# Projecting attention's q and k together in seven half-size products

## The chip, the cores and the metric

The program runs on one core of a Trainium2 chip. The metric is the time of one execution on the device in microseconds. The engines are called by the profile's names: PE (TensorE, the matmuls), DVE (VectorE), ACT (ScalarE), POOL (GpSimd) and SP (SyncE, which issues most of the transfers).

## The reference

One decoder block on 512 tokens of width 1024, all in float32:

```python
h = rmsnorm(x, g_mix)
z = h @ w_in   # q_r,k_r (256 each), v_r,g_r (512 each), q_f,k_f,v_f (512 each), f_f (8), a_r,a_f (1024 each)
o_r = groupnorm(retention(rot(q_r), rot(k_r), v_r)) * g_ret_norm       # chunks of 128 tokens, 4 heads
y_r = (silu(g_r) * o_r) @ w_ret_o
q_f, k_f = rmsnorm(q_f per head, g_q), rmsnorm(k_f per head, g_k)      # 8 heads of 64
y_f = forgetting_attention(q_f, k_f, v_f, logsigmoid(f_f + b)) @ w_fox_o   # causal softmax, bias from cumulative sums of f
x = x + (sigmoid(a_r) * y_r + sigmoid(a_f) * y_f) @ w_out
x = x + (silu(h2 @ w_gate) * (h2 @ w_up)) @ w_down,   h2 = rmsnorm(x, g_ffn)
```

## The kernel before

Each float32 factor is split into a high part (a cast to a shorter format, on ACT) and a low part (the factor less its high part, on DVE); a product of two factors is three matmuls: high by high, high by low, low by high. A *split* of a weight tile of 128 x 1024 is thus one ACT cast (`wh`, line 162) and one DVE subtraction (`wl`, line 163).

The projections of h are done with x scaled by g_mix in `xh`, `xl`; the norm's factor `rstd1` of each token is multiplied in when a result leaves its bank. They come in this order on PE:

1. q_r and k_r together, 512 columns, while x is being loaded.
2. v_r and g_r as a pair, in seven products of half size instead of eight, by a scheme like Strassen's (Winograd's form). The left factor x is cut in four blocks A11, A12, A21, A22 (token halves by alternate row tiles of the width), the weights of the two outputs make the blocks B11, B12, B21, B22 (`blk0` to `blk3`, four buffers of the pool `bp`). Sums of x's blocks (`s1` to `s4`) and sums of weight blocks (line 385, 422) are split and multiplied, and results are added up in the banks `x_`, `y_`, `z_` and in copies `u`. Each product is 24 matmuls of 512 columns (4 row tiles, 2 token tiles, 3 parts).
3. q_f with the 8 forget columns (two column halves of 256 and 264, 96 matmuls each), k_f and v_f (96 matmuls of 512 columns each), by `tok_group`; then the sigmoid gates a_r, a_f (`gates`), then `y_ret`, the projection of retention's output.

The third part does not run by itself. It is a generator `fill`, and a hand-written order takes matmuls worth so many microseconds from it between the steps of retention (rotations on POOL in `ret_rotate`, transposes, scores, values, group norm) and later of the forgetting attention (`fox_...`). The numbers `RF`, `CF`, `PF`, `SF`, `VF`, `TAIL` say how much goes between which steps. While `pinned` is set, PE's instructions keep the order in which they are written; DVE, ACT and POOL are ordered by the framework's scheduler, except where `after` or `queue` chains two instructions. SP issues transfers in the written order while `moves` is set.

Retention runs chunk by chunk (t = 0 to 3): `ret_turn` transposes the rotated q, k (`rot` to `rT`), `ret_scores` makes scores (`sT`) and the state's update (`kv`, `sn`), `ret_values` the outputs in two banks, `ret_norm` statistics and the scaled output `og`, `ret_out` multiplies by the gate `gs` and transposes. q_f and k_f are normalised per head on POOL, turned on DVE (`turn_heads`), written to DRAM and read back head by head (`put_heads`, `get_heads`). In the attention stage the softmax weights are turned on DVE and through DRAM into `pT` (`fox_turn`, `fox_put`, `fox_get`) before `fox_values` multiplies them with v_f.

Of the kernel before, what the change touches and what calls it, by code (L numbers as in the profile page):

```python
# [17 lines left out]
P = 128  # L18
# [34 lines left out]
def block_kernel(ctx: ExitStack, tc, x, xT, c_early, c_tab, c_late, w_qf, w_tok, w_vg, w_a, w_y, w_o, w_gu, w_gl, w_dn, w_dh, out):  # L53
# [88 lines left out]
    RF, CF, PF, SF, LAG = (5.72, 4.64, 5.6, 4.6, 11.2), (3.0, 2.0, 2.26, 4.0), 5.9, (0.63, 0.83, 1.57, 1.4), 2  # L142
# [57 lines left out]
    for k in range(NK):  # L200
# [6 lines left out]
        loads = (load, nc.sync.dma_start(out=raw, in_=w_tok[2, u, :, cs]))  # L207
# [26 lines left out]
    def load_block(b):  # L234
        for v in range(2):
            nc.sync.dma_start(out=blocks[b][:, v, :], in_=w_vg[b, v])
# [33 lines left out]
    def tok_group(src, evac, cuts=(512,), done=(), behind=None):  # L270

        u = 0
        for c, w in enumerate(cuts):
            accs = [bank("acc") for _ in range(NT)]
            kpu = 1024 // (w // 256 * 256)
            for k in range(NK):
                if k % kpu == 0:
                    h, l = done[u] if u < len(done) else split_w(src(u, w * kpu), w * kpu)
                    if behind is not None and u == len(done):
                        after(split_raw.last[0], behind)  # L280
                    u += 1
# [45 lines left out]
    def unit(group):  # L327
        return lambda u, width: w_tok[group, u]

# [7 lines left out]
    def x_sum(n, p, q, op, behind=None):  # L337
# [7 lines left out]
        h = bp.tile([P, 4, HS], F32R, name="sh", tag="sh", bufs=2)  # L345
        l = bp.tile([P, 4, HS], F32R, name="sl", tag="sl", bufs=2)
# [83 lines left out]
    def x_low(n):  # L430
        h = bp.tile([P, 4, HS], F32R, name="sh", tag="sh", bufs=2)
        l = bp.tile([P, 4, HS], F32R, name="sl", tag="sl", bufs=2)
# [26 lines left out]
    t3.append(half(B12, 1))  # L459
    products(x_, t3, s3, False)  # L460
# [4 lines left out]
    b6.append(half(B22, 1))  # L465
    products(z_, b6, s4, False)
# [3 lines left out]
    for v in range(2):  # L470
        sum_half(B11, v, B21)
    b7 = [half(B11, v) for v in range(2)]
    last_low = turn_of[0]
    for tp in range(2):
        queue(tt(out=vr[:, tp, :], in0=y_[tp], in1=us[tp][:, 0, :], op=ALU.add))
    queue_q = split_raw(load_w(w_qf[0, :, :1024]))
    queue(split_raw.last[1])
# [26 lines left out]
    bp.release()  # L504
    orp = tc.alloc_tile_pool(name="orp", bufs=1, side="right")
    sgp = tc.alloc_tile_pool(name="sgp", bufs=1, side="right")


    orh = orp.tile([P, RH, S], F32R, name="orh")
    orl = orp.tile([P, RH, S], F32R, name="orl")  # L510
# [80 lines left out]
    def ret_norm(t):  # L591
# [10 lines left out]
        rsqrt(r4, mv[:, :, 1], 1.0, [P, RH], "n4")  # L602
        og = rwk.tile([P, 512], F32, name="og", tag="og")
        for h in range(RH):
            hs = slice(h * P, (h + 1) * P)
            ts(out=og[:, hs], in0=o[h], scalar1=mv[:, h, 0:1], scalar2=r4[:, h:h + 1], op0=ALU.subtract, op1=ALU.mult)
        ret[t].update(og=og)

    def ret_out(t):
        og = ret[t]["og"]  # L610
        after(gp.tensor_tensor(out=gs[:, t, :], in0=gs[:, t, :], in1=gret, op=ALU.mult), ret[1]["rotated"])
        tt(out=og, in0=og, in1=gs[:, t, :], op=ALU.mult)
# [16 lines left out]
    def head_norm(z, g=None):  # L629
# [3 lines left out]
        def one(t):  # L633
# [3 lines left out]
            if t == NT - 1:  # L637
                r8 = sm.tile([P, NT, FH], F32, name="r8", tag="r8")
                rsqrt(r8.rearrange("p t h -> p (t h)"), s8.rearrange("p t h -> p (t h)"), 1.0 / FD, [P, NT * FH], "n8")
                for u in range(NT):  # L640
                    z3 = z[:, u, :].rearrange("p (h d) -> p h d", h=FH)
                    gp.tensor_tensor(out=z3, in0=z3, in1=r8[:, u, :].rearrange("p (h o) -> p h o", o=1).broadcast_to([P, FH, FD]), op=ALU.mult)
                    if g is not None:
# [916 lines left out]
```

## Time and profile before

| | |
|---|---|
| median of 3 runs | 682.74 us (682.62 to 683.54) |
| profiled execution | 682.73 us, span 680.9 us |
| granted PE clock | 0.999 |
| PE matmul busy | 673.2 us, 3399 records |
| DVE / ACT / POOL busy | 535.5 / 351.0 / 76.2 us |

A row of the timeline gives the start, the duration, the engine, the line of the kernel, the operation, `out<-in` tiles, and in brackets the idle time before it with what ended it. Rows of one engine can overlap by their pipeline, so the distance between two starts is the better price. In the stretches the columns are the length, then busy time and instructions of PE, PEld, DVE, ACT and POOL, the granted clock, the DMA share and GB/s. A wait's row gives the total, the times and the longest.

### The profile page before, as it was taken

Reading aid. Unit: us, or ns where it says so; the run is one execution under the profiler, and the core shown is the slowest. Engines: PE = TensorE matmul, PEld = TensorE weight load, DVE = VectorE, ACT = ScalarE, POOL = GpSimd, SP = SyncE. Lnnn points to the kernel's source line nnn. Section 1 sums busy time; section 2 is a strip of 40 time slices with the busy share of each in tenths; the row PEclk is TensorE's granted clock in tenths of the full one; section 3 lists DMA queues with packets and bytes.
Section 4 is the critical chain, followed back from the end, with each engine's and each line's share of the span. In section 5 each row is a group of like instructions: output and inputs, shape, how many; then the busy total and the mean of one; then the engine's idle time right before and its main releaser. Section 6 shows DMA issues by size and latency. Waiting matters only on the chain.

```text
span 680.9 us, 9401 instructions
## 1 busy us (share of the span) xinstructions
PE 673.2 (99%) x3399; PEld 564.3 (83%) x3399; DVE 535.5 (79%) x865; ACT 351.0 (52%) x516; POOL 76.2 (11%) x96
## 2 busy tenths in 40 slices
PE   8999999999999999999999999999999999999998
PEld 6888997888886778788888888888888898888998
DVE  6899567777688674596989998989999888556794
ACT  6767452433464445254576655564646474343341
POOL 0013945101122210000130000000000000000000
PEclk9999999999999999999999999999999999999999
DMA  8910312624657886337511516445362513554221
GB/s 277 420 53 32 125 63 61 218 86 163 202 169 217 268 270 208 107 111 278 216 63 49 199 32 191 114 145 153 88 179 59 154 63 81 143 145 159 93 94 63
DMA packets 82223, 98.94 MB, mean 145 GB/s; under 512 B 52472, under 2 KB 59256, under 8 KB 81408
## 3 DMA queue, kind: packets, MB, share of 16 engines
q1 hardware_dynamic: 81392, 97.27, 44.8%
q10 hardware_dynamic: 784, 1.06, 0.6%
q8 instruction: 27, 0.44, 0.3%
q14 instruction: 20, 0.16, 0.1%
HBM read 81.97 MB, written 9.52 MB: 134 GB/s over the span
## 4 chain that ended last, share of the span: by engine, by line
PE 79%; DVE 1%; DMA 1%; issue 1%; ACT 1%; SPq 0%; DVEq 0%; ACTq 0%
PE acc L82 62%; PE sc L82 12%; PE tp L82 5%; DMA pT<-pd 1%; ACT ps L1058 0%; DVE ps L1059 0%; PE tp L85 0%; SPq L72 0%; DVE b L1067 0%; DVE wl L163 0%; DVE psq L751 0%; ACT us L1221 0%; DVE us L1271 0%; DVE orl L189 0%; DVE hl L1115 0%
## 5 line engine op out<-in xcount | busy, mean ns | idle before, releaser
L82 PE MATMUL acc<-ps,xfh 128*128 128x512 f32 (+1 forms) x576 | 166.6, 372 | 0.3 <-ACT us L1180 0.3
L82 PEld LDWEIGHTS acc<-ps,xfh 128*128 128x128 f32 x576 | 105.2, 188 | 19.1 <-ACT us L1180 0.5
L1058 ACT CAST ps<-b 128x1024 fp32r<-128x1024 f32 (+1 forms) x84 | 82.4, 981 | 59.9 <-DVE b L1067 26.7
L1059 DVE TENSOR_TENSOR ps<-b,ps 128x1024 fp32r<-128x1024 f32 (+1 forms) x84 | 94.3, 1135 | 20.1 <-ACT ps L1058 18.9
L82 PE MATMUL acc<-ps,xfl 128*128 128x512 f32 (+1 forms) x288 | 106.9, 371 | 0.0
L162 ACT CAST wh<-raw 128x1024 fp32r<-128x1024 f32 (+1 forms) x44 | 46.0, 1049 | 84.1 <-PE acc L82 42.2
L163 DVE TENSOR_TENSOR wl<-raw,wh 128x1024 fp32r<-128x1024 f32 (+1 forms) x44 | 56.5, 1288 | 24.0 <-ACT wh L162 24.0
L82 PEld LDWEIGHTS acc<-ps,xfl 128*128 128x128 f32 x288 | 54.3, 188 | 9.4
L1067 DVE TENSOR_TENSOR b<-b,b 128x1024 f32<-128x1024 f32 (+1 forms) x48 | 52.1, 1125 | 0.0
L82 PE MATMUL acc<-xh,wh 128*128 128x512 f32 x128 | 50.8, 397 | 0.0
L82 PE MATMUL acc<-wh,xh 128*128 128x512 f32 (+2 forms) x144 | 50.3, 350 | 0.0
L82 PE MATMUL acc<-xl,wh 128*128 128x512 f32 x128 | 50.0, 390 | 0.0
L82 PE MATMUL acc<-xh,wl 128*128 128x512 f32 x128 | 49.9, 390 | 0.0
L82 PE MATMUL acc<-wh,xl 128*128 128x512 f32 (+2 forms) x144 | 49.3, 343 | 0.0
L82 PE MATMUL acc<-wl,xh 128*128 128x512 f32 (+2 forms) x144 | 49.3, 342 | 0.0
L82 PE MATMUL acc<-hl,ps 128*128 128x512 f32 x168 | 40.4, 389 | 0.0
L82 PEld LDWEIGHTS acc<-hl,ps 128*128 128x128 f32 x168 | 31.5, 188 | 6.6
L1180 ACT COPY us<-acc 128x512 f32<-128x512 f32 (+1 forms) x48 | 26.1, 550 | 16.3 <-PE acc L82 15.3
L1106 DVE TENSOR_TENSOR ps<-raw,ps 128x1024 fp32r<-128x1024 f32 x14 | 17.1, 1220 | 18.8 <-ACT ps L1103 18.8
L82 PEld LDWEIGHTS acc<-wh,xh 128*128 128x128 f32 x144 | 27.2, 189 | 3.6 <-DVE sT L562 0.2
L82 PEld LDWEIGHTS acc<-wh,xl 128*128 128x128 f32 x144 | 27.2, 189 | 3.2
L82 PEld LDWEIGHTS acc<-wl,xh 128*128 128x128 f32 x144 | 27.2, 189 | 2.9
(302 smaller groups left out, 1438.8 us busy)
## 6 DMA issues: line engine op xcount, KB each, us to landing
b<-in_w_gu_dram SPq DMA_DIRECT2D x40, 512.0 KB, 4.2
raw<-in_w_a_dram SPq DMA_DIRECT2D x16, 512.0 KB, 4.5
raw<-in_w_dn_dram SPq DMA_DIRECT2D x14, 512.0 KB, 4.0
pd<-psq SPq DMA_DIRECT2D x8, 640.0 KB, 4.5
pT<-pd SPq DMA_DIRECT2D x32, 160.0 KB, 4.5
pf<-squares SPq DMA_DIRECT2D x160, 32.0 KB, 1.9
blk<-in_w_vg_dram SPq DMA_DIRECT2D x8, 512.0 KB, 10.0
raw<-in_w_tok_dram SPq DMA_DIRECT2D x8, 512.0 KB, 3.2
```

Of the source, the lines that this page charges most:

```text
L82: in_order(nc.tensor.matmul(o, **kw))
L162: split_raw.last = (nc.scalar.copy(out=h[:, :width], in_=raw[:, :width]), tt(out=l[:, :width], in0=raw[:, :width], in1=f32(h)[:, :width], ...
L163: tt(out=l[:, :width], in0=raw[:, :width], in1=f32(h)[:, :width], op=ALU.subtract))
L1058: part.cast = nc.scalar.copy(out=h, in_=raw)
L1059: low = tt(out=l, in0=raw, in1=f32(h), op=ALU.subtract)
L1067: queue(tt(out=raws[g][b][v], in0=raws[g][b][v], in1=raws[g][c][v], op=ALU.add))
L1106: tt(out=l, in0=raw, in1=f32(h), op=ALU.subtract)
L1180: copy = nc.scalar.copy(out=u_(tp, slot), in_=os[tp][:, :w])
```

## The change

q_f and k_f become a second pair of outputs and are projected by the same seven-product scheme, with weight blocks C11, C12, C21, C22 (`w_qk`) loaded into the four block buffers when the first pair is done with them. The left factors (blocks and sums of x in two parts, `s1` to `s4`) are those of values and gate, kept in four buffers instead of two. The products run in the generator `pair_group`, which prepares each half of a weight block (sum and split) one product ahead. The forget columns move from q_f to v_f, which now takes the two column halves. Combining the quarters of q and k takes subtractions and multiply-adds on DVE and scaled copies on ACT. k is normalised, turned and stored before q. The group norm's scaling moves from DVE (`ts`, line 606) to ACT. The block pool stays until the pair is done, so retention's output buffers are made later. The amounts of filling change.

```diff
-    RF, CF, PF, SF, LAG = (5.72, 4.64, 5.6, 4.6, 11.2), (3.0, 2.0, 2.26, 4.0), 5.9, (0.63, 0.83, 1.57, 1.4), 2
+    RF, CF, PF, SF, LAG = (5.72, 5.64, 5.0, 4.2, 2.5, 14.0), (5.2, 1.0, 2.26, 4.0), 5.9, (0.63, 0.83, 1.57, 1.4), 2
...
-        h = bp.tile([P, 4, HS], F32R, name="sh", tag="sh", bufs=2)
-        l = bp.tile([P, 4, HS], F32R, name="sl", tag="sl", bufs=2)
+        h = bp.tile([P, 4, HS], F32R, name="sh", tag="sh", bufs=4)
+        l = bp.tile([P, 4, HS], F32R, name="sl", tag="sl", bufs=4)
...
+    C11 = load_block(1, 0, w_qk)
     products(x_, t3, s3, False)
...
-    queue_q = split_raw(load_w(w_qf[0, :, :1024]))
-    queue(split_raw.last[1])
+    pair_parts = [half(C11, 0)]
...
         rsqrt(r4, mv[:, :, 1], 1.0, [P, RH], "n4")
+        ret[t]["mean"] = stt(out=mv[:, :, 0], in0=mv[:, :, 0], scalar=-1.0, in1=r4, op0=ALU.mult, op1=ALU.mult)
         og = rwk.tile([P, 512], F32, name="og", tag="og")
         for h in range(RH):
-            ts(out=og[:, hs], in0=o[h], scalar1=mv[:, h, 0:1], scalar2=r4[:, h:h + 1], op0=ALU.subtract, op1=ALU.mult)
+            act(out=og[:, h * P:(h + 1) * P], in_=o[h], func=AF.Identity, scale=r4[:, h:h + 1], bias=mv[:, h, 0:1])
...
+    def pair_group():
+        r = [rstd1[:, t:t + 1] for t in range(NT)]
+        z_, x_ = ([bank("acc") for _ in range(2)] for _ in range(2))
...
+        def k_early():
+            for t in range(2):
+                stt(out=kf[:, t, :], in0=z_[t], scalar=r[t], in1=kf[:, t, :], op0=ALU.mult, op1=ALU.subtract)
+            for t in range(2):
+                knorm(t)
+        def k_late():
+            for t in range(2):
+                act(out=qf[:, t + 2, :], in_=x_[t], func=AF.Copy, scale=r[t + 2])
+                tt(out=kf[:, t + 2, :], in0=kf[:, t + 2, :], in1=qf[:, t + 2, :], op=ALU.subtract)
+            for t in range(2):
+                knorm(t + 2)
+        def q_early():
+            for t in range(2):
+                stt(out=qf[:, t, :], in0=y_[t], scalar=r[t], in1=qf[:, t, :], op0=ALU.mult, op1=ALU.add)
+            for t in range(2):
+                qnorm(t)
...
+        steps = [(C11, None, "x", x_block(A11), True, first_quarter), (C11, C12, "z", s1, True, fourth_quarter), (C11, C22, "x", s2, False, second_quarter),
+                 (C22, None, "z", s4, False, k_early), (C12, C22, "x", s3, False, k_late), (C21, None, "y", x_block(A12), True, q_early),
+                 (C11, C21, "x", x_block(A22), False, q_late)]
+        lows = [split_raw.last[1]] * 2
+        def prepare_half(i):
+            if i < 2 * len(steps):
+                block, other = steps[i // 2][:2]
+                if other is not None:
+                    add_to(block, i % 2, other, lows[-2])
+                pair_parts.append(split_raw(block[:, i % 2, :]))
+                lows.append(split_raw.last[1])
+            elif not ready:
+                ready.append(split_raw(begun.pop(0)))
...
     pinned[0] = True
-    fill = Fill(tok_group(lambda u, width: w_qf[u, :, :width], evac_qf, (256, 264), (queue_q,), turn_act[0]),
-                tok_group(unit(1), evac_kf), tok_group(unit(0), evac_to(vf, AF.Copy)), gates(0), gates(1), gates(2), gates(3), *(y_ret(mp) for mp in range(4)))
+    fill = Fill(pair_group(), tok_group(lambda u, width: w_vf[u, :, :width], evac_vf, (256, 264)),
+                gates(0), gates(1), gates(2), gates(3), *(y_ret(mp) for mp in range(4)))
...
+    fill(RF[5])
     ret_rotate(0)
     fill(RF[0])
```

How it moves instructions, first on DVE at the end of the first pair. In the names, `vr` and `gs` are the first pair's results, `blk0_518` is C11 (and what is summed into it), `blk3_559` C12, `blk2_591` C22, `wl` low parts, `wide` a copy for transposing the norm's factors. Before:

```order
L475 TENSOR_TENSOR vr_581<-sc_476,u_375 128x512
L475 TENSOR_TENSOR vr_581<-sc_477,u_376 128x512
L163 TENSOR_TENSOR wl_598<-raw_595,wh_597 128x1024
L493 TENSOR_TENSOR gs_582<-acc_315,u_375 128x512
L493 TENSOR_TENSOR gs_582<-acc_316,u_376 128x512
L495 TENSOR_TENSOR gs_582<-u_375 128x512
L495 TENSOR_TENSOR gs_582<-u_376 128x512
L259 COPY wide_580<-rstd1_86 128x512
L163 TENSOR_TENSOR wl_724<-raw_654,wh_723 128x1024
L163 TENSOR_TENSOR wl_814<-raw_656,wh_813 128x1056
```

And after, from the last of the `gs` on:

```order
L499 TENSOR_TENSOR gs_588<-u_376 128x512
L385 TENSOR_TENSOR blk0_518<-blk0_518,blk3_559 128x1024
L163 TENSOR_TENSOR wl_664<-blk0_518,wh_663 128x1024
L261 COPY wide_586<-rstd1_86 128x512
L385 TENSOR_TENSOR blk0_518<-blk0_518,blk3_559 128x1024
L163 TENSOR_TENSOR wl_669<-blk0_518,wh_668 128x1024
L163 TENSOR_TENSOR wl_686<-blk0_518,wh_685 128x1024
L385 TENSOR_TENSOR blk0_518<-blk0_518,blk2_591 128x1024 x2
L163 TENSOR_TENSOR wl_705<-blk0_518,wh_704 128x1024
L163 TENSOR_TENSOR wl_722<-blk0_518,wh_721 128x1024
```

What stands there now is an unbroken row of sums and splits of 128 x 1024; the rows up to the last `gs` are the same as before.

Next DVE again, at the end of the pair, where the last product's second half (`wl_955`) is prepared; `kf`, `qf` are k and q, `s8` the sums of squares per head, `n8` the steps of their inverse root, `blk1_602` is C21. After:

```order
L163 TENSOR_TENSOR wl_938<-blk0_518,wh_937 128x1024
L634 TENSOR_REDUCE s8_654<-sq_895 128x8
L385 TENSOR_TENSOR blk0_518<-blk0_518,blk1_602 128x1024
L124 TENSOR_SCALAR n8v_899<-s8_654 128x32
L127 TENSOR_SCALAR n8y_900<-n8v_899 128x32
L691 SCALAR_TENSOR_TENSOR qf_648<-acc_934,rstd1_86,qf_648 128x512
L128 TENSOR_SCALAR n8y_900<-n8y_900 128x32
L691 SCALAR_TENSOR_TENSOR qf_648<-acc_935,rstd1_86,qf_648 128x512
L130 SCALAR_TENSOR_TENSOR n8a_901<-n8y_900 128x32
L163 TENSOR_TENSOR wl_955<-blk0_518,wh_954 128x1024
```

Before, the splits stand nearly alone at that point of the retention:

```order
L163 TENSOR_TENSOR wl_1060<-raw_836,wh_1059 128x1024
L571 COPY sn_834<-sc_829 128x256
L163 TENSOR_TENSOR wl_1090<-raw_890,wh_1089 128x1024
L551 TENSOR_TENSOR rT_895<-rT_895,cl_308 128x256
L655 SCALAR_TENSOR_TENSOR fz_649<-acc_809,rstd1_86,ce_84 128x8
```

Between the sum for the last half and its split there are now six other instructions, two of them combinations of q that wait for the sixth product.

Last PE at the values of the first chunk (`sc<-vr,sT`), with the next chunk's scores and state behind them. After:

```order
L82 MATMUL sc_1021<-vr_587,sT_918 128x128 x2
L82 MATMUL sc_1022<-vr_587,sT_918 128x128 x2
L82 MATMUL tp_1028<-rT_978 128x128 x2
L82 MATMUL tp_1029<-rT_978 128x128 x2
L82 MATMUL sc_1021<-vr_587,kz_843 64x128 x4
L82 MATMUL acc_661<-wh_954,xh_118 128x512
L82 MATMUL acc_661<-wh_954,xl_119 128x512
L82 MATMUL acc_661<-wl_955,xh_118 128x512
```

Before, the same group has a matmul of k behind it:

```order
L82 MATMUL tp_1009<-rT_895 128x128 x2
L82 MATMUL tp_1010<-rT_895 128x128 x2
L82 MATMUL sc_1002<-vr_581,kz_761 64x128 x4
L82 MATMUL acc_1055<-wh_1059,xh_118 128x512
L82 MATMUL acc_1055<-wl_1060,xh_118 128x512
L82 MATMUL acc_1055<-wh_1059,xl_119 128x512
```

So the first chunk's values now stand in the middle of the last product of the pair, six matmuls ahead of v's first.

More of the change, by code (lines that the diff above doesn't have):

```diff
@@ L206, in block_kernel @@
             nc.scalar.copy(out=cold[:, 0:1], in_=cold[:, 1:2])
-        loads = (load, nc.sync.dma_start(out=raw, in_=w_tok[2, u, :, cs]))
+        loads = (load, nc.sync.dma_start(out=raw, in_=w_tok[u, :, cs]))
         if k == 2:
@@ L232, in block_kernel, with load_block @@
     blocks = [bp.tile([P, 2, 1024], F32, name=f"blk{b}") for b in range(4)]
-    def load_block(b):
+    def load_block(b, to=None, src=w_vg):
+        to = blocks[b] if to is None else bp.tile([P, 2, 1024], F32, name=f"blk{to}")
         for v in range(2):
-            nc.sync.dma_start(out=blocks[b][:, v, :], in_=w_vg[b, v])
+            nc.sync.dma_start(out=to[:, v, :], in_=src[b, v])
+        return to
     load_block(1)
@@ L278, in tok_group @@
                     h, l = done[u] if u < len(done) else split_w(src(u, w * kpu), w * kpu)
-                    if behind is not None and u == len(done):
-                        after(split_raw.last[0], behind)
+                    if u == 1:
+                        after(split_raw.last[0], fox["qout"])
                     u += 1
@@ L901, in block_kernel @@
     nc.vector.tensor_copy(out=cs, in_=cps[:, 0:NT * FH].rearrange("p (t h) -> p t h", t=NT))
-    get_heads(kf)
+    while turn_next.n < 9:
+        turn_next()
+    fill(CF[0])
+    ret_out(NT - 1, orh, orl)
     rwk.release()
```

147 lines of the change are left out of this document (91 added, 56 removed).

## Prediction

> **What bounds the kernel now.** I read the page's busy shares first, then the waits of the matmul engine over the whole span, then the stretches around the change.
>
> ```profile
> PE 673.2 (99%) x3399; PEld 564.3 (83%) x3399; DVE 535.5 (79%) x865; ACT 351.0 (52%) x516; POOL 76.2 (11%) x96
> PE tp L82 <- DMA pT<-pd: 1.3, 1, 1.3
> PE tp L82 <- DVE orl L189: 0.6, 1, 0.6
> ...
> PE acc L82 <- DVE wl L163: 0.4, 1, 0.4
> 60.00:80.00 20.00, 20.00 (x145) 18.68 (x144) 14.21 (x14) 13.56 (x21) 17.92 (x18) 1.00 0.26 84
> 80.00:100.00 20.00, 20.00 (x156) 18.41 (x153) 11.95 (x34) 8.59 (x14) 12.91 (x14) 1.00 0.22 80
> 100.00:120.00 20.00, 19.39 (x107) 15.80 (x106) 16.15 (x53) 5.73 (x7) 9.67 (x8) 1.00 0.30 91
> ```
>
> TensorE is the bound nearly everywhere: its waits behind the start come to some 2.5 us, and the granted clock is 1.00 in the stretches. VectorE (third busy figure of a stretch) has 14.2, 12.0 and 16.2 of 20 us to do between 60 and 120. So the change is worth what it takes from TensorE, less what VectorE cannot deliver in time, because that stretch is where all its work is added. GpSimd (fifth figure) is unusually busy there, 17.9 of 20.
>
> **The gain.** One matmul, and what retention puts between:
>
> ```profile
> 61.19 0.39 PE L82 MATMUL acc<-wh,xh 128*128 128x512 f32 x1
> 66.63 0.28 PE L82 MATMUL acc<-wh,xh 128*128 128x256 f32 x1
> ...
> 73.10 0.60 PE L85 MATMUL tp<-ctab,wide 128*128 128x128 f32 x4
> ...
> 73.89 0.36 PE L82 MATMUL acc<-wh,xh 128*128 128x256 f32 x1
> ...
> 79.46 0.72 PE L82 MATMUL tp<-rT 64*128 64x128 f32 x8
> 80.70 0.39 PE L82 MATMUL acc<-wh,xh 128*128 128x264 f32 x1
> ...
> 92.52 1.05 PE L82 MATMUL sc<-vr,sT 128*128 128x128 f32 x8
> 94.74 0.50 PE L82 MATMUL acc<-wh,xh 128*128 128x512 f32 x1
> ```
>
> From 61.19 to 66.63 lie the 24 matmuls of one product of the first pair: 0.2267 us each, 5.44 a product. From 66.63 to 73.10 lie 54 of 256 columns: 0.12 each. Before, q is 192 half-width matmuls (two halves of 96), k 96 and v 96 full ones. After, q and k are 7 x 24 = 168 full ones and v takes over q's halves with the forget columns. The halves cost the same either way, so 192 full ones become 168: 24 x 0.2267 = **5.44 us** less. The order lists 3281 matmuls against 3305, so they are gone.
>
> **VectorE's side.** Before, these columns need 12 splits of about 1024 wide (4 each for q, k, v). Now there are 14 for the pair and 4 for v, 8 sums of blocks and 6 combinations of quarters, and most of it comes first.
>
> ```profile
> 56.60 2.35 DVE L422 TENSOR_TENSOR blk<-blk,blk 128x1024 f32<-128x1024 f32 x2
> 59.00 2.38 DVE L163 TENSOR_TENSOR wl<-blk,wh 128x1024 fp32r<-128x1024 f32 x2
> 61.29 1.28 DVE L475 TENSOR_TENSOR vr<-sc,u 128x512 f32<-128x512 f32 x2
> 62.49 1.60 DVE L163 TENSOR_TENSOR wl<-raw,wh 128x1024 fp32r<-128x1024 f32 x1
> ...
> 67.01 0.83 DVE L259 COPY wide<-rstd 128x512 f32<-128x512 f32 x1
> 70.33 3.25 DVE L163 TENSOR_TENSOR wl<-raw,wh 128x1024 fp32r<-128x1024 f32 x2 [2.48 <-ACT wh L162]
> ...
> 76.66 2.13 DVE L163 TENSOR_TENSOR wl<-raw,wh 128x1056 fp32r<-128x1056 f32 x1 [0.83 <-ACT wh L162]
> 61.46 0.74 POOL L529 TENSOR_TENSOR ta<-rz,cl 128x256 f32<-128x256 f32 x1 [18.15 <-DVE wl L163]
> ...
> 76.39 7.02 POOL L611 TENSOR_TENSOR gs<-gs,cl 128x512 f32<-128x512 f32 x4
> ```
>
> The two splits from 59.00 to 61.29 take 1.15 each while GpSimd is idle. Once GpSimd's rotations start at 61.46 the same operation takes 1.52 (1.60 less the 0.08 by which a row overlaps the next) and 1.62 (half of 3.25), so a rotation in the way costs about 0.45. Beside GpSimd's 512-wide products (76.39) it takes 2.13, so about 0.95 more. Operations with one input in PSUM keep 0.60 (61.29 to 62.49).
> The Trainium skill (SBUF — State Buffer, Who interferes with whom) says that a VectorE instruction with two SBUF inputs and a GpSimd one that reads SBUF lock each other out, the second waiting for the whole first. The trace agrees in kind. If all of each GpSimd operation were waited for, the time would be 685.7 (second rival); without any lock 676.4 (first).
>
> VectorE has no idle in the new order from 67.01 on, so I add its queue and compare it with TensorE's need. Up to 67.01 it stands as before.
> - *To the last half for the fifth product*: 15 sums and splits x 1.15 = 17.3; the wide copy 0.83; GpSimd's rest of two rotations, the start of the third and four products get between them, 9 x 0.45 + 4 x 0.95 = 7.9. Ends at 92.9. On the way the second half of the first product is ready at 70.2, wanted at 66.63 + 2.72 + 0.45 = 69.8 (third matmul of its half); the first half of the second (the copy, a sum and a split, with their waits) at 74.2, wanted at 72.9 after that; of the third (four more operations at 1.6) at 80.6, wanted at 79.6. Stalls: 0.4 + 1.3 + 1.0 = **2.7**.
>
> ```profile
> L636 DVE TENSOR_REDUCE s<-sq 128x8 f32<-128x512 f32 x6 | 4.1, 681 | 0.5 <-ACT sq L635 0.4
> L551 DVE TENSOR_TENSOR rT<-rT,cl 128x256 f32<-128x256 f32 x4 | 3.3, 824 | 1.3 <-ACT rT L550 1.3
> ...
> L562 DVE TENSOR_TENSOR sT<-tp,cl 128x256 f32<-128x256 f32 x6 | 2.2, 416 | 1.5 <-PE tp L82 1.4
> L598 DVE BATCH_NORM_STATS2 bs<-sc 128x6 f32<-128x128 f32 x8 | 2.0, 282 | 0.0
> 120.16 0.16 DVE L130 SCALAR_TENSOR_TENSOR n4a<-n4y 128x4 f32<-128x4 f32 x1
> 121.94 1.36 DVE L606 TENSOR_SCALAR og<-sc,mv,r 128x128 f32<-128x128 f32 x4
> 111.92 0.71 DVE L676 STREAM_TRANSPOSE zsq<-qf 128x512 f32<-128x512 f32 x1 [0.54 <-POOL qf L644]
> 123.82 0.68 DVE L612 TENSOR_TENSOR og<-og,gs 128x512 f32<-128x512 f32 x1
> ```
>
> - *To the second half of the seventh product* (durations less that 0.08): 2 sums and 4 splits 6.9; 6 combinations x 0.60 = 3.6; 4 reductions 2.4; one rT 0.8, two sT 0.75, one sn 0.4; five small steps 0.6; two rotations 0.9. Sum 16.4: ready at 109.3. TensorE without stalls wants it at 66.63 + 6 x 5.44 + 2.7 (retention's groups: two of four transposes in 0.79, scores 1.24, four more transposes 0.4, and an estimated 0.1 at each return) + 3.2 = 105.2. So 4.1 late, **1.4** of it new.
> - *To the first chunk's og*: 3 splits 3.4; 4 reductions 2.4; two rT 1.6, two sT 0.75, two sn 0.6; 4 statistics and their means 1.5; 6 small steps 0.7 and 12 more at 0.16 (alone 0.2 each, 120.16 to 121.94), 1.9; three transposes of k at 0.65; og by the gate 0.7; GpSimd's k products 1.4. Sum 16.9: 126.2. TensorE wants it at 66.63 + 38.1 + 5.5 (those, the second scores with the values 2.22, four transposes) + 75 x 0.12 = 119.2. So 7.0 late, **2.9** new.
>
> So 7.0 is given back by then. Behind it VectorE has per chunk of about 15 us some 12 to do, since ScalarE takes the four scalings of og (1.36 a chunk, the row at 121.94) and the pair's work is over; I cost the later chunks at nothing, and the cover is 10.7 us of v matmuls against a chain of about 7.5. Ends of this term: 0, if GpSimd always yields (the chain is then 10 shorter), and 9.5 with the whole lock.
> ScalarE's 6 more splits at 1.05 lie beside VectorE's slower ones: nothing. The loads of the new blocks wait for the old blocks' buffers, the first free at about 53, and are wanted from 61: nothing. The forget columns come some 40 us later, and their chain has 22 us of gate matmuls before its sums: nothing.
>
> **The attention stage.**
>
> ```profile
> 215.02 2.37 PE L82 MATMUL tp<-pT,vf 128*64 128x512 f32 x14 [1.27 <-DMA pT<-pd]
> 260.32 1.74 SPq L72 DMA_DIRECT2D pT<-pd  x4
> 262.11 1.24 SPq L72 DMA_DIRECT2D rw<-rd  x2
> 275.89 2.38 PE L82 MATMUL sc<-pT,vf 128*64 128x512 f32 x16
> rw<-rd SPq DMA_DIRECT2D x8, 128.0 KB, 4.9
> ```
>
> The first values wait 1.27 for transposed weights; 99 matmuls instead of 96 now lie between the first scores and them, 3 x 0.2267, so I take **0.6** off (ends: all 1.27, or 1 more). I also take half of the 0.6 for orl, **0.3**, since its queue differs. The last values have 12 matmuls less in front (117 for 129), 2.7 us; their last transfer is in at 262.11 + 1.24 + 4.9 = 268.3 and they run at 275.89, so 7.6 of cover becomes 4.9: nothing.
>
> **Sum.** -5.44 + 7.0 - 0.6 - 0.3 = +0.7. The profiled execution took 682.73 (span 680.9 and 1.8 around it), the median is 682.74: **683.4 us**, which is no change: about 0.2%, 1.4 us, is what a measurement of this kernel can tell.
>
> **Rivals.**
> 1. *VectorE keeps up.* GpSimd rather than VectorE waits, or half of its operations fall beside PSUM ones. For it: 18 us of VectorE idle before in 60 to 130. Against: 1.52 and 1.62 for 1.15. With half the delay the chain ends 5 earlier and 2 are given back: 682.7 - 5.4 + 2 - 0.9 = 678.4; with none 676.4; with only the middle stall left 680.5.
> 2. *The whole lock (slower).* Every GpSimd operation holds VectorE for its full 0.74: 1.89 a split in the first three products, eight in the chain to the third, 8 x 0.29 = 2.3 more: 685.7. It decides if a split in 67 to 82 takes over 1.75; the rows at 62.49 and 70.33 speak against. By the Trainium skill's rule (SBUF — State Buffer, Who interferes with whom) this is what should come.
> 3. *The end of attention runs dry (slower).* If the last transposed weights come more than 4.9 later relative to the scores, each us more costs one; 2 more gives 685.4. Against: fewer weight loads are left for that stage.
> That the matmuls are not saved is out: the order shows them gone.
>
> **How the numbers follow.** Forecast (681.4 to 684.1) 0.35; the first rival 0.33; the whole lock 0.2, a longer chain to og by over 1 us 0.06, the end of attention 0.06. Faster 0.33, same 0.35, slower 0.32. The range 679.0 to 686.5 leaves out the case of no delay at all and the worst sums; the forecast's own is 681.4 to 684.1.
>
> **What would show it.** In the new profile: TensorE waits on wl (L163) at the first three products and in the seventh, 4 us together, and on og's gate product (L610) at its first turn, 2 to 3 us; splits of 1.5 to 1.6 between 67 and 80; VectorE busy over 19 of 20 between 60 and 120; the wait for pT under 1.3. I am wrong if VectorE idles there, or if TensorE's waits between 66 and 130 are under 4 or over 9 us.

## The result and the profile after

The changed kernel takes 694.96 us (median of 4 runs, 692.32 to 695.41) against 682.7: ratio 1.0169 [1.0141, 1.0196]. By the medians it is 12.3 us slower. The forecast was 683.4 (679.0 to 686.5). The profiled run is the fastest of the four, 692.32 with a span of 690.5; the working below accounts for that run's 9.6 us over the span before. What made the other three 2.2 to 3.1 us longer is not in a trace.

Page, waits of the matmul engine and stretches of the changed kernel:

```profile
PE 674.8 (98%) x3375; PEld 562.1 (81%) x3375; DVE 561.9 (81%) x873; ACT 363.1 (53%) x540; POOL 88.3 (13%) x96
PE acc L82 <- DVE wl L163: 5.9, 6, 2.2
PE acc L82 <- DVE fz L657: 2.8, 1, 2.8
PE sc L82 <- DMA pT<-pd: 1.2, 1, 1.2
...
60.00:80.00 20.00, 18.34 (x80) 14.49 (x78) 20.00 (x18) 13.08 (x18) 17.92 (x14) 1.00 0.29 114
80.00:100.00 20.00, 19.15 (x98) 15.07 (x97) 19.95 (x15) 11.87 (x16) 17.39 (x13) 1.00 0.00 1
100.00:120.00 20.00, 17.20 (x89) 13.64 (x88) 19.71 (x45) 9.09 (x13) 8.44 (x9) 0.91 0.09 28
120.00:140.00 20.00, 20.00 (x176) 19.42 (x176) 18.30 (x51) 8.11 (x15) 7.95 (x8) 1.00 0.63 197
140.00:160.00 20.00, 17.20 (x109) 15.16 (x108) 12.93 (x35) 10.01 (x17) 2.85 (x3) 0.91 0.34 112
```

VectorE (third busy figure) has no idle left from 60 to 120, as forecast, and TensorE (first) now has gaps in four of the five stretches. Two things are new: a single wait of 2.8 for `fz`, the copy of the forget columns, which the prediction had costed at nothing, and two stretches whose granted clock is 0.91 where it was 1.00.

Where the 9.6 us arise shows at two marks, the first score of the attention stage and the first matmul of w_out. Before, and then after:

```profile
184.64 0.39 PE L82 MATMUL tp<-tk,tq 128*128 128x512 f32 x1
...
304.84 0.39 PE L82 MATMUL acc<-mgh,wh 128*128 128x512 f32 x1
```

```profile
198.59 0.39 PE L82 MATMUL tp<-tk,tq 128*128 128x512 f32 x1
...
314.42 0.39 PE L82 MATMUL acc<-mgh,wh 128*128 128x512 f32 x1
```

The changed order has 33 gate matmuls more ahead of the first score (33 x 0.2267 = 7.5 us). So 13.95 - 7.5 + 5.44 = 11.9 us are lost up to there, and in the attention stage, 115.8 for 120.2 long, 7.5 - 4.4 = 3.1. With the 5.44 gained: 11.9 + 3.1 - 5.44 = 9.6. Behind w_out's first matmul nothing changes.

The 11.9 fall into two pieces. The first is the one forecast, VectorE's queue behind the splits; at the seventh product (timeline, TensorE, then VectorE's split that it waits for):

```profile
109.36 0.40 PE L82 MATMUL acc<-wh,xl 128*128 128x512 f32 x1
111.91 0.79 PE L82 MATMUL acc<-wl,xh 128*128 128x512 f32 x1 [2.15 <-DVE wl L163]
112.50 0.63 PE L82 MATMUL acc<-wh,xh 128*128 128x512 f32 x1
```

```profile
110.64 1.21 DVE L163 TENSOR_TENSOR wl<-blk,wh 128x1024 fp32r<-128x1024 f32 x1
```

The matmul at 111.91 comes 2.55 after the one ahead of it, 2.32 more than the usual 0.2267, and the next ones are 0.59 and 0.43 apart instead of 0.23: behind the pause TensorE runs slowly. The stretches of 3 us give the granted clock (the figure behind GpSimd's):

```profile
109.00:112.00 3.00, 0.82 (x3) 0.39 (x3) 3.00 (x8) 2.00 (x3) 0.85 (x2) 0.90 0.00 0
112.00:115.00 3.00, 3.00 (x11) 2.62 (x12) 3.00 (x8) 0.63 (x1) 0.00 (x0) 0.53 0.02 5
115.00:118.00 3.00, 3.00 (x26) 2.33 (x26) 2.81 (x17) 0.50 (x1) 1.81 (x2) 1.00 0.58 183
```

Taken by single microseconds the clock is 0.50 from 112 to 114. From 111.91 to the matmul at 116.50, behind the scores and the state, TensorE needs 4.59; in the run with matmuls of zeros below, whose clock stays full, the same takes 3.25 (112.64 to 115.89), so the slow clock costs about 1.3 here.

The second piece comes at the end of v, where the first gate product takes over a bank that `fz` must empty. TensorE, then the queue of VectorE ahead of `fz`, then GpSimd:

```profile
145.84 0.28 PE L82 MATMUL acc<-wh,xl 128*128 128x264 f32 x1
148.92 0.79 PE L82 MATMUL acc<-xh,wh 128*128 128x512 f32 x1 [2.80 <-DVE fz L657]
149.51 0.63 PE L82 MATMUL acc<-xl,wh 128*128 128x512 f32 x1
```

```profile
137.45 0.93 DVE L124 TENSOR_SCALAR n4v<-mv 128x4 f32<-128x4 f32 x1
138.41 0.97 DVE L127 TENSOR_SCALAR n4y<-n4v 128x4 int32<-128x4 int32 x1
139.41 0.97 DVE L128 TENSOR_SCALAR n4y<-n4y 128x4 int32<-128x4 int32 x1
140.42 1.21 DVE L130 SCALAR_TENSOR_TENSOR n4a<-n4y 128x4 f32<-128x4 f32 x1
141.66 1.21 DVE L131 TENSOR_TENSOR n4a<-n4a,n4v 128x4 f32<-128x4 f32 x1
142.90 0.16 DVE L132 SCALAR_TENSOR_TENSOR n4y<-n4a,n4y 128x4 f32<-128x4 f32 x1
...
146.08 0.69 DVE L610 TENSOR_TENSOR og<-og,gs 128x512 f32<-128x512 f32 x1 [1.64 <-ACT og L604]
...
147.50 1.23 DVE L163 TENSOR_TENSOR wl<-raw,wh 128x1024 fp32r<-128x1024 f32 x1 [0.39 <-ACT wh L162]
```

```profile
132.86 2.99 POOL L645 TENSOR_TENSOR qf<-qf,r 128x512 f32<-128x512 f32 x2 [12.05 <-ACT wh L162]
135.81 2.54 POOL L647 TENSOR_TENSOR qf<-qf,cl 128x512 f32<-128x512 f32 x2
138.31 2.04 POOL L645 TENSOR_TENSOR qf<-qf,r 128x512 f32<-128x512 f32 x2
140.32 2.53 POOL L647 TENSOR_TENSOR qf<-qf,cl 128x512 f32<-128x512 f32 x2
```

Five steps of four elements a partition take 0.93 to 1.21 us each, where the sixth takes 0.16. They start 0.96 to 1.24 apart, which is GpSimd's pace (2.04/2 to 2.53/2 for one of its products of q), and from the moment its last product ends, at 142.85, they are short. The five lose about 4.4 us. The rest of the second chunk's norm, its `og`, a rotation and a split stand behind them and `fz` behind these, so it starts at 148.65 while v's last matmul is at 145.84. The gap is 2.96 more than usual. Behind it the matmuls are slow again (0.43 to 0.59 apart, the clock 0.50 from 149 to 152): from 148.92 to the seventh gate matmul, at 152.44, it takes 3.52, and 1.94 (146.34 to 148.28) in the run below with all of q's products held, whose clock is full there. So some 4.5 are lost here, and the first piece is the other 7.4.

### The profile page after: what moved, and what is told of

Same layout as the page of the kernel before. It is cut to its first block, busy times and chain, and to the rows that moved or that the text cites. A ratio compares the mean times of both kernels' runs of the same rounds, so it can differ in the third digit from the quotient of the medians.

```text
span 690.5 us, 9398 instructions
## 1 busy us (share of the span) xinstructions
PE 674.8 (98%) x3375; PEld 562.1 (81%) x3375; DVE 561.9 (81%) x873; ACT 363.1 (53%) x540; POOL 88.3 (13%) x96
## 4 chain that ended last, share of the span: by engine, by line
PE 78%; DVE 10%; DMA 4%; issue 3%; ACT 3%; SPq 1%; ACTq 0%; DVEq 0%
PE acc L82 60%; PE sc L82 12%; PE tp L82 5%; DVE wl L163 3%; DVE blk L385 2%; DMA pd<-psq 1%; ACT wh L162 1%; DMA xf<-in_xT_dram 1%; DMA blk<-in_w_vg_dram 1%; DVE ps L1143 1%; ACT ps L1142 1%; ACT junk L380 0%; DMA raw<-in_w_tok_dram 0%; DMA pT<-pd 0%; PE tp L85 0%
## 5 line engine op out<-in xcount | busy, mean ns | idle before, releaser
L162 ACT CAST wh<-raw 128x1024 fp32r<-128x1024 f32 (+1 forms) x36 | 37.7, 1048 | 39.8 <-PE acc L82 13.8
L163 DVE TENSOR_TENSOR wl<-raw,wh 128x1024 fp32r<-128x1024 f32 (+1 forms) x36 | 44.5, 1235 | 12.7 <-ACT wh L162 11.8
L163 DVE TENSOR_TENSOR wl<-blk,wh 128x1024 fp32r<-128x1024 f32 x28 | 40.0, 1444 | 2.1 <-ACT wh L162 2.0
L162 ACT CAST wh<-blk 128x1024 fp32r<-128x1024 f32 x28 | 29.2, 1048 | 19.8 <-DVE blk L385 10.4
L82 PE MATMUL acc<-wl,xh 128*128 128x512 f32 (+2 forms) x104 | 34.4, 331 | 2.6 <-DVE wl L163 2.6
L82 PE MATMUL acc<-wh,xh 128*128 128x512 f32 (+2 forms) x104 | 34.9, 335 | 0.6 <-ACT wh L162 0.4
L82 PE MATMUL acc<-wh,xl 128*128 128x512 f32 (+2 forms) x104 | 33.9, 326 | 0.0
L82 PEld LDWEIGHTS acc<-xh,wh 128*128 128x128 f32 x128 | 24.4, 191 | 7.4 <-DVE fz L657 3.0
```

The costliest lines, as they stand in the source:

```text
L82: in_order(nc.tensor.matmul(o, **kw))
L162: split_raw.last = (nc.scalar.copy(out=h[:, :width], in_=raw[:, :width]), tt(out=l[:, :width], in0=raw[:, :width], in1=f32(h)[:, :width], ...
L163: tt(out=l[:, :width], in0=raw[:, :width], in1=f32(h)[:, :width], op=ALU.subtract))
```

## The experiments

Every ratio is against the kernel before, run beside it on the same chip. The changed kernel, run again as the control:

> The changed kernel unaltered, so that its profile and the others stand on one chip. All theories expect the same waits as in its first profile (three products 3.0 together, seventh product 2.3, forget columns 2.9) and a ratio to the kernel before of 1.014 to 1.020.

1.0170 [1.0143, 1.0198], 694.71 us. Its profiled run again waits 6.2 on `wl` and 2.6 on `fz`. The slow clock falls differently: it lasts from 111 to 118 at the seventh product (0.50 in the stretch 114 to 117), and behind `fz` the clock is 1.00.

**Is it GpSimd that makes the small steps slow?** q's products are held until the second chunk's norm is through (`held(a, b)` in these diffs stands for a dependency that makes a wait for b). In the first version only the first product was:

```diff
-            for u in range(NT):
-                gp.tensor_tensor(out=z3, in0=z3, in1=r8 ...)
+                first = gp.tensor_tensor(out=z3, in0=z3, in1=r8 ...)
+                if u == 0:                     # second version: for every u
+                    held(first, ret[1]["mean"])
...
```

> The changed kernel, with one thing moved: GpSimd's eight products that normalise q wait until the second chunk's group norm is through on VectorE (its last small step), instead of starting when their own factors are ready at 132.9. Theory (lock): in the changed kernel five of the small steps of that norm took 0.93 to 1.21 instead of 0.16 because they alternate with these products; that made the norm 4.5 us late, with it ScalarE's og, VectorE's og product and, behind them in the same queues, the copies that empty the banks of v and of the forget columns, for which TensorE waits 2.96 at 145.84 and then runs some 2 us slower. So here the small steps take 0.16 each, the wait is under 0.5, no slowed matmuls follow, and the time is 4 to 5 us less than the changed kernel's. Rival (the queue's order): the forget columns are late because they are issued behind a gate product and a split; then the small steps get fast but the wait stays over 2 us and the time is within 1 us of the changed kernel's.

1.0112 [1.0097, 1.0128]. The order let six of the eight products go ahead and only the last two waited, so three of the small steps were still slow. The wait for `fz` fell to 1.1, and the matmuls behind it were at full clock. With every product held:

> The first experiment again, this time with all eight of GpSimd's products on q held behind the second chunk's norm (there six of the eight still ran beside it). Theory (lock): no small step of that norm over 0.25; the wait for the forget columns is at most the 1.1 of the first experiment, and the time 3 to 5 us under the changed kernel's on this chip. Rival (queue's order): the wait stays at 1.0 to 1.3 though the norm is 2 us earlier, because the copies stand behind a gate product that waits for ScalarE, a product on the keys and a split.

1.0096 [1.0069, 1.0124], 4.4 us less than the control. VectorE's small steps and TensorE's wait:

```profile
137.21 0.17 DVE L124 TENSOR_SCALAR n4v<-mv 128x4 f32<-128x4 f32 x1
137.41 0.17 DVE L127 TENSOR_SCALAR n4y<-n4v 128x4 int32<-128x4 int32 x1
...
146.34 0.50 PE L82 MATMUL acc<-xh,wh 128*128 128x512 f32 x1 [0.47 <-DVE fz L665]
```

The same instructions at the same place take 0.17 once GpSimd is quiet, and the wait falls from 2.80 to 0.47. That shows the cause of the `fz` piece. For its size the marks are better than the medians. The first score is at 194.41, 4.2 ahead of the first profile: 2.6 by the first gate product, 1.6 by the clock behind it. Against the control (197.88) it is 3.5, of which 2.1 is the wait. The attention stage then takes 118.05, longer than the first profile's 115.83, so that the profiled spans differ by 2.0 only (688.5 for 690.5). That the medians differ by 4.4 is close to the 4.5 above partly by chance.

**Are the splits slow because of GpSimd?** The rotation of the second chunk is held until the sixth half (the third product's second) is split:

```diff
-        if t == 0:
-            held(first, last_low)
+        if t == 0 or t == 1:
+            held(first, last_low if t == 0 else fox["pair", 5])
...
```

> The changed kernel, with GpSimd's rotation of the second chunk (and so its gate products and later rotations, which stand behind it) held back until VectorE has the second half of the pair's third product in two parts. Theory (lock): with GpSimd idle from about 67.5 on, sums and splits take 1.15 instead of 1.65 to 1.75, the waits at the first three products (0.6, 1.37 and 1.0) fall to under 1.0 together, and the time falls by 2 to 4 us; the lock comes back later, beside the fourth to sixth products, where VectorE has more slack, so the wait in the seventh product may stay. Rival (too much work): VectorE has more sums and splits than fit in whatever GpSimd does; the durations fall but the waits at the first three products stay over 2 us together.

1.0105 [1.0077, 1.0133]. A row of sums and splits, and TensorE at the seventh product:

```profile
73.56 2.35 DVE L385 TENSOR_TENSOR blk<-blk,blk 128x1024 f32<-128x1024 f32 x2
75.95 2.38 DVE L163 TENSOR_TENSOR wl<-blk,wh 128x1024 fp32r<-128x1024 f32 x2
...
109.74 0.50 PE L82 MATMUL acc<-wl,xh 128*128 128x512 f32 x1 [3.22 <-DVE wl L163]
```

Yes: 1.2 each instead of 1.68, and the waits at the first three products are gone. But 1.1 of it comes back at the seventh, whose half is late by VectorE's queue as a whole (without the sums, in the next run, there is no wait there), and the `fz` wait stays (2.8). The profiled runs differ by 0.9 in the span, the ratios by more; the rest lies in the changed kernel's longer runs.

**Is VectorE's sum of work the limit?** All eight sums of blocks are left out (so the products are of other blocks; matmuls and splits are as many):

```diff
-                if other is not None:
-                    add_to(block, i % 2, other, lows[-2])
```

> The changed kernel without the eight sums of weight blocks in the pair (the products then multiply the unsummed blocks): VectorE's work there falls by eight operations of 1.15 to 2.3. Theory (VectorE's queue is full from 67 on, by work and lock together): the waits at the first three products and in the seventh vanish, so does most of the og wait; up to the end of v TensorE gains 7 to 9 us; the wait for the forget columns, which comes from the second norm, stays at 2.5 to 3; the time is 6 to 9 us under the changed kernel's. Rival (GpSimd alternates with whatever VectorE does, so that the lock expands with the gaps): the splits get no shorter and at least half of the waits stay.

1.0046 [1.0031, 1.0061], 7.8 us less than the control. The waits at the first three products and at the seventh are gone. The `fz` wait is 2.8 as before and 2.5 on a later `wl` are left, so even without any sums the kernel is 3.1 us slower than before: what the prediction did not see outweighs the gain by itself.

**What is the slow clock worth?** Nine matmuls of zeros are added into the bank ahead of the seventh product's late half, so that TensorE does not pause:

```diff
+                        if n == 6 and j == 2 and tp == 0 and m == 2:
+                            for _ in range(9):
+                                mm(os[tp], lhsT=warm[:, 0:P], rhs=warm, start=False, stop=False)
```

> The changed kernel, with nine matmuls of zeros (512 columns) put into TensorE's order at the place where it waits 2.32 us for the second half of the seventh product; they add zero to an open sum. Theory (clock): the pause itself makes the following matmuls run at 0.43 instead of 0.2267 for some us; with TensorE kept busy by zeros the spacing after them stays 0.23, the granted clock of 108 to 120 rises from about 0.8 to over 0.95, and the time falls by 1 to 2 us although the wait for VectorE is the same. Rival (other cause, say VectorE's and ScalarE's load): the spacing after the place is 0.43 as before and the time is the same or up to 2 us more.

1.0153 [1.0129, 1.0177], the interval overlaps the control's. Stretches and the next turn of TensorE:

```profile
108.00:114.00 6.00, 5.42 (x24) 3.05 (x24) 5.96 (x14) 3.72 (x5) 2.57 (x3) 1.00 0.01 3
...
129.04 0.63 PE L85 MATMUL tp<-ctab,og 128*128 128x128 f32 x4 [1.41 <-DVE og L610]
```

The clock stays at 1.00 and the matmuls behind are 0.23 apart, but what that gains is given back by 129: `og` comes from VectorE's queue at its own time, and TensorE, now earlier, waits 1.41 for it instead of 0.15. So here the slow clock was covered by the later wait. The same was not tried behind `fz`.

**Did moving the group norm's scaling to ScalarE matter?**

```diff
-            act(out=og[:, hs], in_=o[h], func=AF.Identity, scale=r4[:, h:h + 1], bias=mv[:, h, 0:1])
+            ts(out=og[:, hs], in0=o[h], scalar1=mv[:, h, 0:1], scalar2=r4[:, h:h + 1], op0=ALU.subtract, op1=ALU.mult)
```

> The changed kernel with one part undone: the group norm's scaling goes back from ScalarE (four times 128x128, 1.51 a chunk) to VectorE (1.36 a chunk). Theory (VectorE is what TensorE waits for): VectorE's queue between 113 and 146 grows by up to 1.4 a chunk, less the 1.6 us that it idles for ScalarE's og; the first og turn and the forget columns are 0 to 1.4 later each, and the time is 0 to 3 us more. Rival (the crossing to ScalarE and back costs more than the work): the wait at 145.84 shrinks by 0.5 or more and the time falls by 1 to 2 us.

1.0160 [1.0143, 1.0178]: no difference. The wait for `fz` is 2.5, and there is one of 0.8 for `og`.

**All of it moved.** The second chunk's rotation and GpSimd's gate products later, k's squares, sums and products behind the first `og`, q's behind the second norm:

```diff
...
-            for t in range(2):
-                knorm(t)              # and qnorm, likewise, inside the pair
+            if t == 1:                # behind ret_out
+                for u in range(NT):
+                    knorm(u)
+            if t == 2:
+                for u in range(NT):
+                    qnorm(u)
...
```

> The changed kernel with four things moved: the second chunk's rotation behind the third product's split (as in the second experiment); GpSimd's gate products behind the rotations of chunks two and three, the last two behind the second norm; the sums and the norm of k behind the first chunk's gate product, those of q behind the second chunk's norm, GpSimd's products on them accordingly. Theory (VectorE and GpSimd do in 67 to 146 what has no hurry): some 10 us of VectorE's work and most of the lock leave the stretch up to the first og; the waits at the first three products are under 1.0 together, in the seventh product under 1.0, at the forget columns under 1.0, no stretch of slow matmuls; the time is 8 to 11 us under the changed kernel's, 1 to 4 under the kernel before. Rival (the work only moves the wait): q's heads come later by some 15 us or a chunk's norm is late behind the transposes of k, and the time is within 5 us of the changed kernel's.

1.0147 [1.0121, 1.0173]. VectorE, then TensorE:

```profile
128.31 0.71 DVE L754 STREAM_TRANSPOSE zsq<-kf 128x512 f32<-128x512 f32 x1 [1.21 <-POOL kf L655]
```

```profile
142.56 0.50 PE L82 MATMUL acc<-xh,wh 128*128 128x512 f32 x1 [4.27 <-DVE fz L669]
```

All waits up to the end of v are gone (its last matmul is at 138.01), and one of 4.27 for `fz` is the answer: k's transposes, at the head of VectorE's queue, wait for GpSimd, and the second chunk's statistics behind them; the gate product (1.51 beside GpSimd's) and sums of squares then stand ahead of `fz` as well. It is the same queue with another thing at its head. Next, k's transposes go behind `fz`, and k's and q's products behind the second norm:

> As the all-later experiment, but GpSimd's products on k also wait for the second chunk's norm, and the transposes of k stand behind the copies of the forget columns, so that VectorE's queue in front of these holds nothing that waits for GpSimd. Theory (the wait for the forget columns is whatever VectorE's queue holds up in front of them): it falls from 4.3 there to under 1.0, the gain of some 8 us up to the end of v stays, and the time is 8 to 11 us under the changed kernel's, 684 to 687 on a chip where the kernel before takes 684. Rival (the work only moves): q comes later still, the waits of the gate stage behind 150 (5 us there) grow, and the time is within 4 us of the changed kernel's.

1.0151 [1.0131, 1.0170]. `fz` costs 0.8 now, but q's products (146.41 to 155.4) fall beside the third chunk's norm and the sums of the forget columns:

```profile
150.89 1.08 DVE L124 TENSOR_SCALAR n4v<-mv 128x4 f32<-128x4 f32 x1
...
152.90 1.32 DVE L127 TENSOR_SCALAR n4y<-n4v 128x4 int32<-128x4 int32 x1
...
PE tp L85 <- DVE og L613: 2.7, 1, 2.7
```

A third place, the same cause: 0.16 becomes 1.08 to 1.33.

**The attention stage.** `PF`, the filling ahead of the scores, is cut from 5.9 to 3.86, in that last kernel and in the changed kernel alone:

> The kernel of the previous run with nine gate matmuls fewer in front of the first scores (PF 3.86 for 5.9), so that the gates' weight units meet attention's heads in the kernel before's phase (174 gate matmuls before the first score, 6 over a multiple of 24, as 150 there; 183 in the changed kernel). Theory (phase): the waits for wl near 238 (1.0 to 1.7 in the changed kernel, none before) go, 1 to 2 us under the previous run. Rival (amount: too few gate matmuls are left in attention, since 33 more are used before it): the waits move to another unit and the time is within 0.7 us of the previous run's.

> The changed kernel with only PF 3.86 for 5.9. Theory (phase): 1 to 2 us under the changed kernel's, from the wait for wl near 238. Rival (amount): within 0.7 us of it, or more.

1.0076 [1.0063, 1.0088], 4.7 us less than without; and 1.0108 [1.0092, 1.0124], 3.7 less than the control by the medians, which come from two chips (3.4 by the distance to the kernel before beside each). In both the wait on `wl` near 238, of 0.9 in the changed kernel's first profile and 1.5 in its control, is gone. But the 3.7 are not all the number's doing. The profiled run with only `PF` changed is 2.8 shorter than the first profile. Its attention stage takes 116.88, with 24 gate matmuls moved ahead of the first score instead of 33, so it loses 2.1 for 3.1: 1.0 of the 2.8. The other 1.8 lie ahead of the first score (194.70), where the clock behind `fz` stayed at 1.00 this time, as in the control. Does the number do this in any kernel of this kind, by where the gate products stand at the first score? The kernel before with `PF` at 7.94 has 159 gate matmuls ahead of its first score, 15 beyond a whole group of 24, as the changed kernel has with 183:

> The kernel before with PF 7.94 for 5.9: nine gate matmuls more in front of attention's first score (159 for 150), which brings it into the changed kernel's phase (15 over a multiple of 24). Theory (phase: what PF 3.86 won in the changed kernel, 3.7 us of the medians, is the phase and has nothing to do with the pair): 2 to 4 us slower than the kernel before, with a wait for wl or pT between 190 and 260 that is not there now. Rival (amount: the changed kernel has 33 gate matmuls fewer left for attention, and nine of them come back): 9 fewer in the kernel before cost nothing, the time is within 0.7 us.

0.9996 [0.9985, 1.0008]: no. So what the number brings belongs to the changed kernel's own amounts. In the traces it is 1.0 against the first profile and, by the same count, 1.8 against the control, whose attention stage takes 116.66; what else the attention stage loses stays open.

**A version that keeps both apart.** The same kernel with the shorter `PF`, q's sums early and the later gate products behind the first `og`:

> As the run before it with PF 3.86, with three things placed anew: the last two gate products stand behind the first chunk's gate product, the sums of q's squares right behind those of k, and only the small steps of q's norm behind the second chunk's norm, so that GpSimd's products on k and q are over before the third chunk's norm. In that run eight small steps took 1.08 to 1.33 instead of 0.16 from 148.7 to 155.4, and TensorE waited 2.5 for og and 2.4 for a split behind it, then 2.1 for a cast that stood behind late casts of q. Theory (a chain of small steps beside GpSimd is what costs): these waits fall to under 1.5 together and the time by 4 to 7 us, to about 682 to 685, the kernel before's or up to 0.3% less. Rival (VectorE's work itself does not fit): no small step is over 0.3 but waits of 4 us or more remain, on splits, and the time falls by less than 2.

1.0089 [1.0074, 1.0104]: the third `og` waits for nothing, but q's own small steps now stand beside k's products, ahead of `fz`:

```profile
135.94 1.02 DVE L127 TENSOR_SCALAR n8y<-n8v 128x32 int32<-128x32 int32 x1
...
PE acc L82 <- DVE fz L659: 3.5, 1, 3.5
```

Last, k's products start as soon as their factors are ready (128.58 to 132.6, ahead of the second norm at 133.05), and q's go from 139.98 to 150.0, behind it and ahead of the third; two kinds of ScalarE's casts are ordered behind the weights' cast. The edit against the run before it:

```diff
-        nc.scalar.copy(out=h, in_=src)
+        after(nc.scalar.copy(out=h, in_=src), split_raw.last[0])
...
             k8 = head_factors(head_sums(kf, ret[0]["out"]))
+            scale_heads(kf, k8, None, None)
...
-            scale_heads(kf, k8, None, ret[1]["mean"])
```

> As the run before it in the changed kernel, where the small steps of q's norm stood in front of the copies of the forget columns and took 0.97 to 1.02 beside GpSimd's products on k (three of them, and 1.57 for og by the gate): now GpSimd's products on k start as soon as k's factors are there, in front of the second chunk's norm instead of behind it, and two casts of the gates' weights stand on ScalarE in front of the cast of orh and of the first casts of k and q. Theory (chain of small steps beside GpSimd): the wait for the forget columns falls from 3.5 to under 1.0, the waits near 164 and 185 (1.4, 1.8 and 0.3) to under 1.5 together, no stretch of slow matmuls is left, and the time is 683 to 686, within 0.3% of the kernel before. Rival (VectorE's amount of work): the small steps of the second norm or the statistics in front of it get slow instead, or the queue of 118 to 140 ends as late as there, and the time falls by under 2 us.

0.9971 [0.9960, 0.9982], 682.2 us against 683.89: faster than both kernels, by 1.7 us of the 5.44 against the kernel before. Waits and one stretch:

```profile
PE acc L82 <- DVE wl L163: 1.9, 2, 1.3
PE tp L82 <- DMA pT<-pd: 1.0, 1, 1.0
PE acc L82 <- DVE fz L661: 0.2, 1, 0.2
...
100.00:120.00 20.00, 20.00 (x142) 18.05 (x141) 17.44 (x39) 9.46 (x14) 11.80 (x11) 1.00 0.25 82
```

Every small step of the norms but one (0.56, at 110.97) is 0.16 to 0.19 there, and no stretch from 60 to 160 is below full clock. The waits of TensorE behind 60 come to 4.4 us in the profiled run, where they were 2.2 before. That run (682.87) is among the longer of its eleven; what holds the rest of the 5.44 back is not shown. Nor were the moves of rotation, gate products and casts tried in the kernel before, so it is not shown that the 1.7 come from the pair alone.

## Why the prediction was wrong, point by point

In the profiled run the span grew by 9.6 where 0.7 was expected. Of the 8.9 between, 0.4 lie up to 130, 4.5 at `fz` and 4.0 in the attention stage.

- *The gain, 5.44*: right. The matmuls are gone, and the work between the marks adds up with them.
- *Splits of 1.52 to 1.62 beside GpSimd; part to the fifth product ends at 92.9; stalls of 2.7 at products one to three*: nearly right: 1.68, 94.5, and 3.0 by starts. The later rotation shows the cause. The 1.62 was the half of a row whose two splits take 1.54 and 1.78 by themselves; the second, beside GpSimd all the way, was the price that came. The rows of splits:

```profile
72.81 3.43 DVE L163 TENSOR_TENSOR wl<-blk,wh 128x1024 fp32r<-128x1024 f32 x2
...
79.39 5.67 DVE L163 TENSOR_TENSOR wl<-blk,wh 128x1024 fp32r<-128x1024 f32 x3
...
91.68 2.89 DVE L163 TENSOR_TENSOR wl<-blk,wh 128x1024 fp32r<-128x1024 f32 x2
```

- *The second half of the seventh product ready at 109.3, 1.4 new*: mis-sized. It is ready at 111.85 and costs 2.3, with 0.55 for the half ahead of it and about 1.3 of slow matmuls.
- *The first `og` at 126.2, 2.9 new*: it was there at 127.9, but TensorE was by then as late itself, and waits 0.15. The two errors nearly cancel: 7.0 were expected up to 130, and about 7.4 (11.9 - 4.5) were lost. That the sum up to there was right is in part luck.
- *"I cost the later chunks at nothing, and the cover is 10.7 us of v matmuls against a chain of about 7.5"*, and the forget columns *"nothing"*: this is the main step that failed. The chain of a chunk was priced with small steps of 0.2, read where they ran freely; q's eight products of GpSimd, which the new order puts exactly there, make five of them 4.4 us longer. And the cover was looked for behind the forget columns, at the gates' 22 us, while what they hold up is ahead: the bank that the first gate product needs. It cost 4.5 us with the slow clock behind it; holding all of q's products back took the wait from 2.80 to 0.47 and brought the first score 4.2 earlier.
- *The clock*: the sum had no term for it. Its part is the 1.3 at the seventh product and 1.6 of the 4.5 at `fz`.
- *Attention -0.9*: wrong, +3.1. The wait for `pT` is 1.2 as before, the wait for `orl` is gone, and a new one on `wl` near 238 came (0.9); the rest is open, as said.
- *The rivals*: VectorE did not keep up. The whole lock would have needed splits over 1.75 between 67 and 82, 1.89 each. They stood near that line: 1.75 as the rows give them, 1.68 less the overlap, as the prediction counts. Of the three from 79.39 the first two took 1.68 too; the third, from 82.75 beside GpSimd's 512-wide gate products, took 2.23. By the Trainium skill (SBUF — State Buffer, Who interferes with whom) the second of the two fully blocks. The wide splits agree with that only in part: both prices are 0.2 under the sum of the two operations alone (1.15 + 0.74, and 1.15 + 1.28 for a gate product). The small steps, each of which ends as a GpSimd product ends, agree with it fully. Applied to the norm's chain as well as to the splits, that rule would have pointed at the `fz` wait. That the end of attention runs dry did not come: the wait there is 1.2.

The sign that was to show the forecast wrong, waits of TensorE between 66 and 130 under 4 or over 9, did not come: they are 5.3 by their rows. What made it wrong lies outside the stretch that was watched.

## What to carry to other kernels

Price a chain of tiny VectorE instructions by their number, not their size, wherever GpSimd may be reading at the time: each can cost one whole GpSimd operation. For every bank or buffer that is emptied by an engine's in-order queue, read what stands ahead of the emptying instruction in the new order, even when the result itself is wanted much later. And when a stage is filled up, ask where the work that it pushes back (here GpSimd's products of q) will stand, and beside what.

## What the runs showed of the hardware

- A VectorE step of 128x4 to 128x32 takes 0.15 to 0.19 alone and mostly 0.91 to 1.33 beside GpSimd's 128x512 products, in the norms of all of the first three chunks and in q's; steps with one input and a scalar (lines 124, 127) as much as those with two. Sums and splits of 128x1024 start 1.15 to 1.2 apart alone, 1.68 beside GpSimd's 256-wide and 2.23 beside its 512-wide operations.
- Behind most pauses of TensorE of 1.8 us and more the granted clock was 0.50 for 3.4 us, and 512-column matmuls started 0.43 apart; at the seventh product in the control it lasted 6.8. Which pauses were followed by it differs between runs of the same kernel: behind `fz`, 2.80 was (0.50 from 149 to 152) and 2.55 in the control was not, nor 2.78 with only `PF` changed. Pauses of 1.63 and less left it at 1.00 in every run. The Trainium skill (TensorE: Matmul & The Clock Gate, What's actually happening) gives an idle window of about 3.4 us before the rate is halved; pauses shorter than that were enough here.
